# The first stage of a hybrid attention layer written as one fixed order, with value products of 512 columns and matmuls on a cleared tile at the start

## The chip, the cores and the metric

The kernel runs on one core of one Trainium2 chip. The metric is the device time of one execution in microseconds (us). TensorE (PE) does the matmuls and PEld loads their stationary operands; VectorE (DVE), ScalarE (ACT) and GpSimd (POOL) work elementwise; every DMA in this kernel is issued from SyncE's queue (SP). Operands live in on-chip memory, and matmul results in eight banks of PSUM of 128 x 512 fp32 each.

## The reference

One layer of a bidirectional encoder on 1024 tokens of width 1024, fp32. A normalised input `h` is projected once into everything; two kinds of attention run on parts of the projection, and their gated outputs are merged.

```
h = rmsnorm(x, attn_norm_g)
proj = h @ w_in
(c_q, c_kv, k_rope, z_mla, q_dil, k_dil, v_dil, z_dil,
 g_mla, g_dil) = split(proj)              # 256, 128, 32, 512, 3 x 1536, 512, 2 x 1024 columns
a_out = mla_attention(c_q, c_kv, k_rope, positions, ..., w_uq, w_ukv)   # 8 heads, low-rank q and kv
y_mla = (a_out * silu(z_mla)) @ w_o_mla
d_out = dilated_mixture(q_dil, k_dil, v_dil, positions)    # 3 groups of 8 heads, dilations 1, 4, 16
y_dil = (d_out * silu(z_dil)) @ w_o_dil
merged = sigmoid(g_mla + b[:1024]) * y_mla + sigmoid(g_dil + b[1024:]) * y_dil
out = rmsnorm(x + merged @ w_out, final_norm_g)
```

## The kernel before

Every fp32 operand is kept as two parts, a high one rounded to the matmul's format and a low one with the rest (`split`: a cast on ACT for the high part, a subtraction on DVE or POOL for the low one). A product of two such operands is three matmuls, high by high, high by low, low by high (`mm3`, lines 145 to 147).

The run has these stages. (1) *First products* (`latent_proj`): the 416 columns of `w_in` for the latents `c_q`, `c_kv` and `k_rope`, from the transposed input `hTh`/`hTl` (in the profile `at_r`) and the weights `wl_h`/`wl_l`, 8 pieces of 128 tokens, each over 8 pieces of the depth (`kc`): 192 matmuls. The first 512 tokens go depth by depth, as x and weights arrive, the second 512 token piece by token piece. `token_factors` takes the squares of the rows of x (line 276) and the reciprocal norm, as a column (`rcol`) and, by a transpose (line 280) and a trip through DRAM (`s_rs`), as a row `R`; `tables` makes the rotary tables. (2) *Latents* (`latents`): for each half of the tokens the latents are scaled on DVE (line 358), transposed on PE against an identity in `consts` (line 365), split (lines 368, 369), multiplied by the up-projections `uq`, `ukv`, and every result is put into a staging tile `mla_st` of 512 KB and stored to DRAM (`s_qn`, `s_qr`, `s_kn`, `s_kp`, `s_mv`). (3) *Values* (`dil_v`): for each of 3 groups and each of 2 quads of heads, 8 token pieces of 8 x 3 matmuls with 256 columns of value weights (`w_h`, `w_l`), scaled by `rcol` and stored from `dv_st` or `dv_s2`. (4) `block_sums` prepares sums and differences of the input, and `blocks` makes the other projections in 16 items of 7 products ("places") of 12 matmuls of 512 columns, in banks `st_a` to `st_d`; the weights of a place are prepared `LEAD` = 5 places ahead by `block_operand`. (5) Attention and output.

What sets the order: up to `blocks` the Tile framework's scheduler orders the instructions of each engine by a simulated timeline, so latents and value products are mixed as it sees fit; `blocks` and attention stand in a `manual_schedule`, in which each engine follows the order of the code. A tile pool with `bufs=n` gives a name n buffers in turn; the (n+1)th use waits until the first is free. The latents have 2 PSUM banks and 2 staging tiles, the value and first products 6 banks. Weight loads, loads of x, and all stores go through SP's one queue in that order.

```
    def run(self):
                ...
                with tc.tile_pool(name="pj_a", reuse_waits="tile", bufs=NB_A, space=PSUM) as pj, ...
                            self.latent_proj(lp, wl, xp, pj)
                            self.tables(xp)
                            self.token_factors(xp, pl)
                            ...
                                self.latents(up, lp, tp, pl)
                            self.dil_v(0, 0, vp, pj)
                            self.dil_v(0, 1, vp, pj)
```

Of the kernel before, what the change touches and what calls it, by code (L numbers as in the profile page):

```python
# [10 lines left out]
F32 = mybir.dt.float32  # L11
# [28 lines left out]
NB_A = 6  # L40
# [21 lines left out]
class Net:  # L62
# [127 lines left out]
    def constants(self, cp):  # L190
        nc, a = self.nc, self.a
        t = cp.tile([128, 1], F32, name="warm")
        nc.vector.memset(t, 0.0)
        nc.scalar.activation(out=t, in_=t, func=AF.Square)
        c = cp.tile([128, 156], F32, name="consts")
        self.dma(c, a["consts"])
        self.ident, self.ga, self.gq, self.hb, self.iv = c[:, 0:128], c[:, 128:136], c[:, 136:139], c[:, 139:155], c[:64, 155:156]
# [35 lines left out]
    def latent_proj(self, lp, wl, xp, pj):  # L233
# [9 lines left out]
        for half in range(2):  # L243
            ps = [pj.tile([128, 512], F32, name="pj") for _ in range(4)]
            todo = []
            for kc in range(8):
                self.load_x(half, kc, xp)
                if half == 0:
                    raw = wl.tile([128, 416], F32, name="wl_raw", bufs=3)
                    self.dma(raw, a["wl"][kc])  # L250
                    self.split(raw, h[:, kc], l[:, kc], nc.gpsimd if kc % 2 else v)
                for t in range(4):
                    todo.append((kc, t))
            if half:
                todo.sort(key=lambda x: x[1])
            for kc, t in todo:
                ts = slice(512 * half + 128 * t, 512 * half + 128 * t + 128)
                self.mm3(ps[t][:, :416], self.hTh[:, kc, ts], self.hTl[:, kc, ts], h[:, kc], l[:, kc], kc == 0, kc == 7)
            for t in range(4):
                i = 4 * half + t  # L260
                junk = xp.tile([128, 256], F32, name="x_junk", bufs=2)
                nc.scalar.activation(out=junk, in_=ps[t][:, 0:256], func=AF.Square, accum_out=self.lss[:, 0, i:i + 1])
                nc.scalar.activation(out=junk[:, 0:128], in_=ps[t][:, 256:384], func=AF.Square, accum_out=self.lss[:, 1, i:i + 1])
                v.tensor_copy(self.lat[:, i, 0:400], ps[t][:, 0:400])
                v.tensor_copy(self.lat[:, i, 416:432], ps[t][:, 400:416])
            if half == 0:
                v.tensor_scalar(out=self.hb, in0=self.hb, scalar1=0.5, scalar2=None, op0=ALU.mult)

    def token_factors(self, xp, pp):

        nc, a = self.nc, self.a
        ss = xp.tile([128, 8], F32, name="x_ss", bufs=1)
        for t in range(8):
            x = xp.tile([128, D], F32, name="x_in")
            self.dma(x, a["x"][128 * t:128 * t + 128, :])
            nc.scalar.activation(out=x, in_=x, func=AF.Square, accum_out=ss[:, t:t + 1])
        y = self.rsqrt(ss, 1.0 / D, xp, 8)
        nc.vector.tensor_copy(self.rcol, y)
        pt = pp.tile([128, 512], F32, name="pj")
        nc.tensor.transpose(pt[:8, :128], y, self.ident)  # L280
        row = xp.tile([8, 128], F32, name="x_row", bufs=1)
# [5 lines left out]
    def tables(self, tp):  # L287
# [4 lines left out]
        self.dma(pi, a["positions"].partition_broadcast(64))  # L292
        ang = tp.tile([64, S], F32, name="ang", bufs=1)
# [7 lines left out]
        v.tensor_scalar(out=ang, in0=ang, scalar1=PI_LO, scalar2=-PI_LO, op0=ALU.min, op1=ALU.max)  # L301
        cs = tp.tile([64, 2, S], F32, name="cs", bufs=1)
        nc.scalar.activation(out=cs[:, 1], in_=ang, func=AF.Sin)
        v.scalar_tensor_tensor(out=ang, in0=ang, scalar=-1.0, in1=ang, op0=ALU.mult, op1=ALU.max)
        v.tensor_scalar(out=ang, in0=ang, scalar1=-1.0, scalar2=float(np.float32(np.pi / 2)), op0=ALU.mult, op1=ALU.add)
        nc.scalar.activation(out=cs[:, 0], in_=ang, func=AF.Sin)
        self.dma(self.cst, cs)
# [7 lines left out]
    def rope(self, pa, pb, cos, sin, tp):  # L315
# [3 lines left out]
        m = [tp.tile([128, 512], F32, name=f"rope_m{i}") for i in range(4)]  # L319
# [6 lines left out]
    def up_weights(self, lp):  # L326
# [5 lines left out]
        for i in range(3):  # L332
            raw = lp.tile([128, 1024], F32, name="u_raw")
            n = 768 if i < 2 else 1024
            self.dma(raw[:, :n], a["wuq"][:, 768 * i:768 * i + 768] if i < 2 else a["wukv"])
            self.split(raw[:, :n], uh[:, i] if i < 2 else kh, ul[:, i] if i < 2 else kl, nc.gpsimd)
        return uh, ul, kh, kl

    def latents(self, up, lp, tp, pj):

        nc, a = self.nc, self.a
        v = nc.vector
        uh, ul, kh, kl = up
        for half in range(2):
            c512 = slice(half * 512, half * 512 + 512)

            r = self.rcol[:, 4 * half:4 * half + 4]
            sc = tp.tile([128, 2, 4], F32, name="lat_sc")
            for i in range(2):
                v.scalar_tensor_tensor(out=sc[:, i], in0=self.lss[:, i, 4 * half:4 * half + 4], scalar=(0.5, 1.0)[i], in1=r, op0=ALU.mult, op1=ALU.mult)  # L350
                v.tensor_tensor(out=sc[:, i], in0=sc[:, i], in1=r, op=ALU.mult)
            y = self.rsqrt(sc.rearrange("p a b -> p (a b)"), 1.0 / 128, tp, 8)
            for i in range(2):
                v.tensor_tensor(out=y[:, 4 * i:4 * i + 4], in0=y[:, 4 * i:4 * i + 4], in1=r, op=ALU.mult)
# [1386 lines left out]
```

## Time and profile before

| | |
|---|---|
| median of 3 runs | 1227.03 us (1226.45 to 1229.11) |
| the profiled execution | 1229.1 us, its span 1227.1 |
| PE busy in the span | 1204.8 us (98%), 6909 matmuls recorded |
| DVE, ACT, POOL busy | 729.4, 611.9, 579.1 us |
| first matmul | 5.76 us |
| first block product | 224.80 us |

Times in the profile are counted from the start of its span. A row of the waits names the engine and its instruction, what ended its idle time, and then the total, the number and the longest. A row of the timeline has the start, the duration (from issue to the modelled end, so matmuls in a row overlap; what one costs is the distance from its start to the next start), the engine, the line of the kernel, and output <- inputs; in square brackets stands the idle time before it. `at_r` is the transposed input, `pj` a bank of the first stage, `w_h` and `w_l` the weight parts.

### The profile page before, as it was taken

The page shows a single profiled execution, that of the slowest core. Times are in us where ns is not written, and L with a number is a line of the kernel's source. Part 1 is how long each engine was busy: PE and PEld are TensorE (multiplying, and loading weights), DVE is VectorE, ACT ScalarE, POOL GpSimd, SP SyncE. Part 2 cuts the span into 40 slices and gives each one's busy share as a digit, 9 for nine tenths or more (in the row PEclk, how much of TensorE's full clock was granted, in tenths as well). Part 3 has the DMA queues.
Part 4 walks back from the last instruction along what each step waited for, and adds up shares of the span by engine and source line. Part 5 has one row for each costly group of instructions (what it writes and reads, how often), then busy time and mean ns, then how long its engine had stood idle before and what let it go on. Part 6 is the DMA issues. An engine that isn't in the chain of part 4 may idle for free.

```text
span 1227.1 us, 19477 instructions
## 1 busy us (share of the span) xinstructions
PE 1204.8 (98%) x6909; PEld 1061.2 (86%) x6909; DVE 729.4 (59%) x1304; ACT 611.9 (50%) x1284; POOL 579.1 (47%) x490
## 2 busy tenths in 40 slices
PE   8989999999999999999999999999999999999997
PEld 7989999888888888888989898888888888888886
DVE  7483534376566753346666666647667767769442
ACT  6533335443434434446564756546556555654222
POOL 1361218777777777643365633416730101158322
PEclk9989999999999999999999999999999999999999
DMA  9858579356536544286889897965473445235241
GB/s 336 233 160 306 192 288 335 104 146 165 158 106 182 152 132 129 103 239 216 242 231 285 222 296 214 277 181 124 155 194 95 119 104 140 78 112 177 81 154 52
DMA packets 126416, 221.37 MB, mean 180 GB/s; under 512 B 28072, under 2 KB 60400, under 8 KB 121392
## 3 DMA queue, kind: packets, MB, share of 16 engines
q1 hardware_dynamic: 126320, 220.14, 60.4%
q8 instruction: 54, 0.88, 0.3%
q14 instruction: 42, 0.34, 0.1%
HBM read 149.24 MB, written 70.85 MB: 179 GB/s over the span
## 4 chain that ended last, share of the span: by engine, by line
PE 78%; DMA 9%; DVE 3%; ACT 3%; POOL 3%; issue 2%; SPq 1%; ACTq 0%; POOLq 0%; DVEq 0%
PE bank L145 6%; PE bank L147 6%; PE bank L146 6%; PE bank L871 4%; PE st_a L145 2%; PE st_a L147 2%; PE st_a L146 2%; PE st_c L146 2%; PE st_d L146 2%; PE st_d L145 2%; PE st_c L145 2%; PE st_d L147 2%; PE st_c L147 2%; PE bank L896 2%; PE bank L895 2%
## 5 line engine op out<-in xcount | busy, mean ns | idle before, releaser
L152 POOL TENSOR_TENSOR w_l<-w_raw,w_h 128x512 fp32r<-128x512 f32 x188 | 245.8, 1321 | 234.6 <-ACT w_h L151 183.2
L151 ACT CAST w_h<-w_raw 128x512 fp32r<-128x512 f32 x188 | 112.2, 620 | 106.3 <-POOL w_raw L496 90.6
L145 PE MATMUL bank<-at_r,w_h 128*128 128x512 f32 x344 | 141.3, 411 | 0.0
L146 PE MATMUL bank<-at_r,w_h 128*128 128x512 f32 x344 | 134.8, 392 | 0.6 <-POOL at_r L152 0.6
L147 PE MATMUL bank<-at_r,w_l 128*128 128x512 f32 x344 | 135.0, 392 | 0.0
L879 DVE TENSOR_TENSOR at_r<-bank,at_r 128x512 fp32r<-128x512 f32 x128 | 87.8, 687 | 68.0 <-ACT at_r L873 67.5
L873 ACT CAST at_r<-bank 128x512 fp32r<-128x512 f32 x128 | 74.9, 585 | 82.0 <-PE bank L871 81.2
L147 PE MATMUL pj<-w_h,at_r 128*128 128x256 f32 x384 | 109.7, 286 | 0.0
L146 PE MATMUL pj<-w_l,at_r 128*128 128x256 f32 x384 | 109.6, 286 | 0.0
L145 PE MATMUL pj<-w_h,at_r 128*128 128x256 f32 x384 | 109.6, 285 | 0.0
L496 POOL TENSOR_TENSOR w_raw<-w_raw 128x512 f32<-128x512 f32 x64 | 82.9, 1295 | 0.1
L871 PE MATMUL bank<-consts,at_f 128*128 128x128 f32 x512 | 76.8, 272 | 0.5 <-DVE at_r L879 0.5
L147 PEld LDWEIGHTS bank<-at_r,w_l 128*128 128x128 f32 x344 | 64.5, 188 | 14.5
L147 PEld LDWEIGHTS pj<-w_h,at_r 128*128 128x128 f32 x384 | 74.3, 194 | 1.0
L146 PEld LDWEIGHTS pj<-w_l,at_r 128*128 128x128 f32 x384 | 74.3, 193 | 0.8
L145 PEld LDWEIGHTS pj<-w_h,at_r 128*128 128x128 f32 x384 | 74.3, 193 | 0.7
L1144 DVE TENSOR_TENSOR at_r<-bank,at_r 128x512 fp32r<-128x512 f32 x64 | 43.9, 685 | 51.5 <-ACT at_r L1140 51.2
L146 PEld LDWEIGHTS bank<-at_r,w_h 128*128 128x128 f32 x344 | 65.0, 189 | 9.7 <-POOL at_r L152 1.0
L145 PEld LDWEIGHTS bank<-at_r,w_h 128*128 128x128 f32 x344 | 64.9, 189 | 8.8
L896 PE MATMUL bank<-at_r,at_r 128*128 128x256 f32 x256 | 66.9, 283 | 1.4 <-DVE at_r L879 1.4
L895 PE MATMUL bank<-at_r,at_r 128*128 128x256 f32 x256 | 66.9, 282 | 0.0
L1125 ACT ACTIVATE at_f<-at_f,at_f 128x256 f32<-128x256 f32 x128 | 64.1, 504 | 3.8 <-DVE at_f L1118 3.7
(325 smaller groups left out, 3328.2 us busy)
## 6 DMA issues: line engine op xcount, KB each, us to landing
w_raw<-wt SPq DMA_DIRECT2D x48, 512.0 KB, 3.7
at_r<-s_dq SPq DMA_DIRECT2D x32, 512.0 KB, 8.1
s_dk<-dq_st SPq DMA_DIRECT2D x80, 128.0 KB, 2.3
s_dv<-dv_st SPq DMA_DIRECT2D x32, 256.0 KB, 3.4
s_dq<-dq_st SPq DMA_DIRECT2D x64, 128.0 KB, 2.4
zt<-s_gt SPq DMA_DIRECT2D x32, 256.0 KB, 3.5
w_raw<-wv SPq DMA_DIRECT2D x12, 512.0 KB, 5.7
at_r<-s_dk SPq DMA_DIRECT2D x8, 576.0 KB, 10.3
```

Of the source, the lines that this page charges most:

```text
L145: mm(out, lh, rh, start=start, stop=False, skip_group_check=skip)
L146: mm(out, lh, rl, start=False, stop=False, skip_group_check=skip)
L147: return mm(out, ll, rh, start=False, stop=stop, skip_group_check=skip)
L151: self.nc.scalar.copy(out=h, in_=raw)
L152: sub.tensor_tensor(out=l, in0=raw, in1=h.bitcast(F32), op=ALU.subtract)
L496: self.nc.gpsimd.tensor_tensor(out=b[out], in0=b[x], in1=b[y], op=ALU.subtract)
L871: self.nc.tensor.transpose(pt[:, o:o + 128], self.P[k, b][:, 128 * kc:128 * kc + 128], self.ident)
L873: self.nc.scalar.copy(out=h, in_=pt)
L879: self.nc.vector.tensor_tensor(out=l, in0=pt, in1=h.bitcast(F32), op=ALU.subtract)
L895: mm(out, vv[:, kc], ph[:, x], start=kc == 0, stop=False)
L896: mm(out, vv[:, kc], pl[:, x], start=False, stop=kc == 7)
L1125: nc.scalar.activation(out=p, in_=p, func=AF.Exp, scale=-1.0, bias=nm, accum_out=den)
```

## The change

The whole run stands in a `manual_schedule`. `first_products` and `first_stage` replace `latent_proj`, `token_factors`, `dil_v` and the scheduler's mixing.

- The value products have 512 columns: both quads of a group together. `v_part` is half the depth of one token piece, 12 matmuls; 48 parts (`c` = 0 to 47) make the stage. A piece of 512 columns has two parts, which lie some parts apart.
- `latents` becomes a generator of 36 steps. From part 6 on, 1.75 steps are taken behind each part (`LATENTS_BEGIN`, `LATENTS_PACE`). The staging tile has 5 buffers. The scaling of the latents goes to parts 2 to 9, the copy of `R` to part 20 (`token_row`), `block_sums` to part 30 and on, the first five block operands to parts 44 to 47, on DVE.
- PSUM has two pools of 4 banks. The first products use both, then the values one and the latents the other.
- At the beginning PE does ten matmuls of 416 columns on a piece of `wl_h` that DVE clears (`idle`), into a bank that is overwritten later. The first depth piece has its twelve products ordered by operand: 4 high by high, 4 with the low weights, 4 with the low input. The weights' load stands ahead of x's; the cast of this first piece is on DVE. `consts` comes in two parts.
- Value weights are loaded in pieces of 256 KB. The rotary tables' four multiplies by `R` (line 1632), the stores of zeros and the masks' load move into `blocks`. The operands of the block products alternate between two pools by fours instead of by ones.

```
-        for half in range(2):
-            ps = [pj.tile([128, 512], F32, name="pj") for _ in range(4)]
...
+        idle = h[:, 7]
+        v.memset(idle.bitcast(F32), 0.0)
+        for _ in range(10):
+            nc.tensor.matmul(ps[7][:, :416], lhsT=idle[:, 0:128], rhs=idle, start=True, stop=True)
+        for kc in range(8):
+            raw = wl.tile([128, 416], F32, name="wl_raw", bufs=4)
+            if kc == 0:
+                x, c = xp.tile([128, 512], F32, name="x_t", bufs=6), slice(0, 512)
+                self.dma(raw, a["wl"][0])
+                self.dma(x, a["xt"][0, :, 0])
+                v.tensor_copy(h[:, 0], raw)
+                nc.scalar.mul(self.hTh[:, 0, c], x, self.ga[:, 0:1])
...
+                for i, (p, q) in enumerate(((self.hTh, h), (self.hTh, l), (self.hTl, h))):
+                    for t in range(4):
+                        nc.tensor.matmul(ps[t][:, :416], lhsT=p[:, 0, 128 * t:128 * t + 128], rhs=q[:, 0], start=i == 0, stop=False)
+                continue
...
+    def v_part(self, c, pool, tp):
+
+        g, r = divmod(c, 16)
+        part, t = divmod(r, 4)
+        t += 4 * (part // 2)
+        s = (0, 1, 1, 0)[part] ^ (g & 1)
+        begin = part % 2 == 0
+        if begin:
+            self.v_ps[t] = pool.tile([128, 512], F32, name="pj")
+        ps = self.v_ps[t]
+        sl = slice(128 * t, 128 * t + 128)
+        for i in range(4):
+            kc = 4 * s + i
+            self.mm3(ps, self.hTh[:, kc, sl], self.hTl[:, kc, sl], *self.v_w[s, i], begin and i == 0, not begin and i == 3)
...
+            pl = pool(ctx, "pj_l", 4, space=PSUM)
+            pj = pool(ctx, "pj_a", 4, space=PSUM)
...
+            latents = self.latents(next(weights), up, tp, pl)
...
+            for c in range(48):
+                self.v_part(c, pj, vp)
+                g, r = divmod(c, 16)
+                if 2 <= c < 10:
+                    self.latent_scaled(c - 2)
...
+                if c == 20:
+                    self.token_row(tp, pl)
...
+                if c >= LATENTS_BEGIN and latents:
+                    steps += LATENTS_PACE
+                    while steps >= 1 and latents:
+                        steps -= 1
...
+                            next(latents)
...
+                elif later and c >= 30:
+                    next(later, None)
...
+            if x in (2, 3, 4, 5):
+                y, c = (self.cos_d, self.sin_d)[x // 2 - 1], slice(512 * (x % 2), 512 * (x % 2) + 512)
+                self.nc.gpsimd.tensor_tensor(out=y[:, c], in0=y[:, c], in1=self.R[:, c], op=ALU.mult)
```

PE at the very beginning, before: three rows of the start and how they go on (line 145 is high by high, 146 the low weights, 147 the low input).

```order
L145 MATMUL pj<-wl_h,at_8192_r 128x416 x4
L146 MATMUL pj<-wl_l,at_8192_r 128x416
L147 MATMUL pj<-wl_h,at_8192_r 128x416
L146 MATMUL pj<-wl_l,at_8192_r 128x416
L147 MATMUL pj<-wl_h,at_8192_r 128x416
```

And in the changed kernel (lines 265 and 278 are its `first_products`):

```order
L265 MATMUL pj<-wl_h 128x416 x10
L278 MATMUL pj<-wl_h,at_8192_r 128x416 x4
L278 MATMUL pj<-wl_l,at_8192_r 128x416 x4
L278 MATMUL pj<-wl_h,at_8192_r 128x416 x4
L145 MATMUL pj<-wl_h,at_8192_r 128x416
L146 MATMUL pj<-wl_l,at_8192_r 128x416
```

Ten matmuls of the cleared tile now stand ahead, and the low products of the first depth piece are grouped by operand instead of alternating.

PE where the latents' transposes begin, before: `lat` is the scaled latents, `consts` the identity, and the products around it are values of 256 columns.

```order
L145 MATMUL pj<-w_h,at_8192_r 128x256
L146 MATMUL pj<-w_l,at_8192_r 128x256
L365 MATMUL pj<-consts,lat 128x128 x4
L147 MATMUL pj<-w_h,at_8192_r 128x256
L145 MATMUL pj<-w_h,at_8192_r 128x256
L365 MATMUL pj<-consts,lat 64x128 x4
L146 MATMUL pj<-w_l,at_8192_r 128x256
```

In the changed kernel, at the last transposes of the first half and the first up-projections behind them:

```order
L146 MATMUL pj<-w_l,at_8192_r 128x512
L147 MATMUL pj<-w_h,at_8192_r 128x512
L440 MATMUL pj<-consts,lat 64x128 x4
L145 MATMUL pj<-lat_h,uq_h 128x512
L146 MATMUL pj<-lat_l,uq_h 128x512
L147 MATMUL pj<-lat_h,uq_l 128x512
L145 MATMUL pj<-lat_h,uq_h 128x512
L146 MATMUL pj<-lat_l,uq_h 128x512
L147 MATMUL pj<-lat_h,uq_l 128x512
L145 MATMUL pj<-w_h,at_8192_r 128x512
```

The transposes and the up-projections now stand between whole parts of twelve value matmuls of 512 columns, no longer between single matmuls of 256. From the first block product on, PE's order is the same in both kernels.

SP in the first half of the latents, in the changed kernel: stores of the latents (`mla_st`), of the values (`dv_st`) and loads of value weights (`wv`).

```order
L141 DMA s_qn<-mla_st 256x1x512
L141 DMA s_qr<-mla_st 256x1x512
L141 DMA s_dv_68<-dv_st 128x1024
L141 DMA s_kn<-mla_st 256x1x512 x2
L141 DMA s_dv_68<-dv_st 128x1024
L141 DMA s_kn<-mla_st 256x1x512 x2
L141 DMA s_dv_68<-dv_st 128x1024
L141 DMA w_raw<-wv 128x2x256 x4
L141 DMA s_mv<-mla_st 128x1024
```

Before, a value store there was 128x512 (256 KB), twice as many of them, and a load of value weights was 128x1024.

More of the change, by code (lines that the diff above doesn't have):

```diff
@@ L38 @@
 GATES_END = PROJ_BEGIN = 33
-NB_A = 6
+LATENTS_BEGIN, LATENTS_PACE = 6, 1.75
 DIL = (1, 4, 16)
@@ L269, in token_factors, with product @@
-    def token_factors(self, xp, pp):
-        nc, a = self.nc, self.a
-        ss = xp.tile([128, 8], F32, name="x_ss", bufs=1)
[L273 to L276, printed above, removed]
+        ps = {}
+        def product(t, kc):
+            ts = slice(128 * t, 128 * t + 128)
+            self.mm3(ps[t][:, :416], self.hTh[:, kc, ts], self.hTl[:, kc, ts], h[:, kc], l[:, kc], kc == 0, kc == 7)
@@ new lines, in first_products, with load, squares @@
+        for kc in range(8):
+            self.load_x(1, kc, xp)
+        for t in range(4, 8):
+            for kc in range(8):
+                product(t, kc)
+        ss = xp.tile([128, 8], F32, name="x_ss", bufs=1)
+        xs = {}
+        def load(t):
+            xs[t] = xp.tile([128, D], F32, name="x_in")
+            self.dma(xs[t], a["x"][128 * t:128 * t + 128, :])
+        def squares(t):
+            nc.scalar.activation(out=xs[t], in_=xs[t], func=AF.Square, accum_out=ss[:, t:t + 1])
@@ new lines, in first_products @@
+        self.v_load(0, 0)
+        for t in range(3):
+            load(t)
+        next(tables)
+        for t in range(4):
+            squared(t)
+            taken(t)
+        for i in range(4):
+            self.v_split(0, i, nc.gpsimd)
+        for t in range(3):
+            squares(t)
+            if t < 2:
+                load(t + 3)
+        next(tables)
+        squared(4)
+        taken(4)
+        self.v_load(0, 1)
+        for t in range(5, 8):
+            squares(t - 2)
+            load(t)
+            if t == 5:
+                next(tables)
+            if t == 6:
+                for i in range(4):
+                    self.v_split(1, i, nc.gpsimd)
+            squared(t)
+            taken(t)
@@ L277, in token_factors, with token_row @@
+        for t in range(6, 8):
+            squares(t)
+        run_all(tables)
         y = self.rsqrt(ss, 1.0 / D, xp, 8)
-        nc.vector.tensor_copy(self.rcol, y)
+        v.tensor_copy(self.rcol, y)
+        v.tensor_scalar(out=self.hb, in0=self.hb, scalar1=0.5, scalar2=None, op0=ALU.mult)
+    def token_row(self, tp, pp):
+        nc = self.nc
         pt = pp.tile([128, 512], F32, name="pj")
-        nc.tensor.transpose(pt[:8, :128], y, self.ident)
-        row = xp.tile([8, 128], F32, name="x_row", bufs=1)
+        nc.tensor.transpose(pt[:8, :128], self.rcol, self.ident)
+        row = tp.tile([8, 128], F32, name="mla_st", bufs=5)
```

433 lines of the change are left out of this document (245 added, 188 removed).

## The prediction

> **What bounds the kernel now.** I began with the page's table of busy times, to see which engine is full, then cut the span into its stages, then asked what TensorE (PE) waited for in the stages that the change rewrites, and last read single matmuls in the timeline for their steps (start to next start).
>
> ```profile
> span 1227.1 us, 19477 instructions
> PE 1204.8 (98%) x6909; PEld 1061.2 (86%) x6909; DVE 729.4 (59%) x1304; ACT 611.9 (50%) x1284; POOL 579.1 (47%) x490
> ```
>
> PE is the bound of the whole run: 98% busy, 22 us idle. The rows below are the stages: start, first products, value products beginning, latents, the rest of the values, blocks, attention with output. Columns: stretch and its length, busy time and count on PE, PEld, DVE, ACT and POOL, granted clock, DMA share, GB/s.
>
> ```profile
> 0.00:5.76 5.76, 0.00 (x1) 0.00 (x1) 0.68 (x3) 2.66 (x5) 0.72 (x5) 1.00 0.61 191
> 5.76:44.80 39.04, 39.04 (x194) 38.41 (x195) 28.07 (x41) 30.86 (x68) 13.70 (x11) 1.00 0.90 319
> 44.80:82.00 37.20, 32.31 (x248) 31.57 (x247) 25.93 (x96) 13.25 (x33) 17.10 (x12) 0.91 0.71 192
> 82.00:180.00 98.00, 97.55 (x705) 92.17 (x704) 43.18 (x71) 37.36 (x70) 22.68 (x18) 1.00 0.68 251
> 180.00:224.80 44.80, 42.78 (x357) 42.58 (x356) 18.53 (x15) 27.22 (x52) 35.34 (x26) 1.00 0.82 275
> 224.80:531.00 306.20, 306.20 (x1344) 253.36 (x1345) 169.60 (x271) 126.89 (x240) 217.50 (x179) 0.99 0.50 139
> 531.00:1227.10 696.10, 686.91 (x4070) 603.14 (x4068) 443.39 (x810) 373.62 (x822) 272.01 (x243) 1.00 0.61 174
> ```
>
> The blocks (306 us) have no idle PE at all, and PE's order there and in attention stays as it is; only what lies ahead of 224.80 can move. There PE stands still 5.76 us at the start and a little more later. Its waits up to 240 us, in total, times and longest:
>
> ```profile
> PE pj L145 <- ACT wl_h L151: 5.8, 1, 5.8
> PE pj L365 <- DVE lat_l L369: 3.4, 1, 3.4
> PE st_a L145 <- ACT dv_s L457: 2.0, 1, 2.0
> PE pj L365 <- DVE lat L358: 1.2, 1, 1.2
> PE pj L145 <- DVE mla_st L152: 0.4, 1, 0.4
> PE pj L280 <- DVE rs_y L210: 0.3, 1, 0.3
> ```
>
> After the start that is 3.4+2.0+1.2+0.4+0.3 = 7.3 us: the latents' transposes waiting for the scaled latents, and the first block product waiting for a PSUM bank that the value products still hold. Two of these stalls are followed by a slower clock. The clock column of short stretches shows it (the first row's 1.00 can't be believed: the steps there are long, see below):
>
> ```profile
> 5.76:11.17 5.41, 5.41 (x16) 5.16 (x17) 4.00 (x7) 4.32 (x8) 1.21 (x1) 1.00 0.99 365
> 11.17:44.80 33.63, 33.63 (x180) 33.25 (x179) 24.07 (x35) 26.54 (x62) 12.49 (x10) 1.00 0.89 311
> 73.97:79.43 5.46, 5.46 (x26) 5.33 (x27) 3.25 (x6) 1.67 (x3) 4.64 (x5) 0.50 0.91 273
> 224.80:229.62 4.82, 4.82 (x14) 3.83 (x15) 0.69 (x1) 1.78 (x4) 3.10 (x3) 0.65 0.44 135
> 229.96:232.00 2.04, 2.04 (x10) 1.69 (x9) 0.00 (x0) 0.34 (x1) 1.29 (x1) 1.00 1.00 365
> ```
>
> **A, the value products at 512 columns.** 1152 matmuls of 256 columns become 576 of 512, the same products summed in the same way. A step of 256 columns: in the stretch 180.00:224.80 PE was busy 42.78 us with 357 of them, 0.1198 us each. A step of 512 where the weights also change at every matmul: the 9 whole steps of 229.96:232.00 take 2.04 us, 0.2267 each. So 1152 x 0.1198 = 138.0 becomes 576 x 0.2267 = 130.6: -7.4. The latents' matmuls of 512 are a second witness and step more slowly, 4 steps in 0.93 us, 0.2325 each:
>
> ```profile
> 82.14 0.40 PE L145 MATMUL pj<-lat_h,uq_h 128*128 128x512 f32 x1
> 83.07 0.39 PE L146 MATMUL pj<-lat_l,uq_h 128*128 128x512 f32 x1
> ```
>
> By that, 576 x 0.2325 = 133.9, a gain of only 4.1. I take the blocks' row, since their moving operand is also a split weight block that streams in while PE goes on; the ends are -7.4 and 0 (no gain at all, should the new operands add what the halved count saves). The Trainium skill's page "TensorE: Matmul & The Clock Gate" (part 1, "Wait — 56ns, not 53.3ns?") speaks against this term: a warm step is N/2.4 GHz plus some 2.5 ns, so by it 576 fewer matmuls give an estimated 1.4 us. The trace disagrees for these matmuls: 2 x 0.1198 - 0.2267 is 12.9 ns for each one dropped, five times that.
>
> **B, the stalls.** The change writes the order out: the latents' 36 steps begin behind the seventh value part and go in at 1.75 steps a part, so every transpose has value products ahead of it that need nothing from DVE; the last values use a bank ring of their own, so the first block product needs no bank of theirs. The 7.3 us go: -7.3. New waits are not in the trace of before. Their lower end is 0. Their upper end is a row-sum for the staging tile of the latents (idle time of engines before they could write it, by what ended it, us and times):
>
> ```profile
>   DMA s_qn<-mla_st: 9.5, 3
>   DMA s_kn<-mla_st: 9.1, 5
>   DMA s_qr<-mla_st: 4.9, 3
>   DMA s_mv<-mla_st: 3.1, 2
> ```
>
> That is 26.6 us in which ACT waited for a store to land, with two buffers. ACT was idle there anyway and PE did not feel it (97.55 of 98.00 us busy). Now there are five buffers, so a store may land three products later. I take +1.0, near the lower end, since PE's own idle in that stretch is 0.45 us even with two.
>
> What is late next: first the reciprocal norms at the beginning. Eight squares of x rows run on ACT behind the first products:
>
> ```profile
> L276 ACT ACTIVATE x_in<-x_in 128x1024 f32<-128x1024 f32 x8 | 8.5, 1063 | 2.9 <-DMA x_in<-x 2.9
> ```
>
> With PE at the sum below, first products end near 42.5 and the first transpose comes seven parts (7 x 12 x 0.2267 = 19.0 us) later, at 61.6; 8.5 us of squares, the norm and two scalings have to fit into that and do by a few us. Second, the transfers: each stored piece is 512 KB, 14 of them per half, with four value stores of 512 KB and 1 MB of value weights between: 10.5 MB in about 35 us (72 to 107), 300 GB/s. The trace's densest stretch (40 slices of 80 to 106 us) and one such store there:
>
> ```profile
> GB/s 25 50 353 139 359 321 101 170 343 353 337 107 6 148 262 0 0 0 35 416 391 407 410 340 25 6 0 378 410 403 410 413 397 19 403 388 6 25 186 406
> s_qn<-mla_st SPq DMA_DIRECT2D x4, 512.0 KB, 3.1
> ```
>
> Peaks are about 410 GB/s, so 300 fits, and a landing of 3.1 us is under the four products that a ring of five allows. On SP's queue all stores and weight loads stand in one line: a load of value weights that waits for POOL's split of the previous ones holds back the stores behind it, and the copy of the norm row after the twentieth part waits for its own store. That is where the +1.0 would come from, and more if it goes badly.
>
> **C, the half clock after the stalls.** 73.97:79.43 ran at 0.50, 5.46 x 0.50 = 2.7 lost; 224.80:229.62 at 0.65, 4.82 x 0.35 = 1.7 lost. Without the stalls both go: -4.4. It goes only if no new wait of about 2 us stands in their place: the second one followed an idle of 2.0 us. The Trainium skill's page "TensorE: Matmul & The Clock Gate" (part 1, "What's actually happening") has the clock fall after an idle window of about 3.4 us; here the trace disagrees, with 2.0 us being enough.
>
> **D, the beginning.** In 5.76:11.17 the 16 matmuls take 5.41 us, 0.338 each; in 11.17:44.80 the 180 take 33.63, 0.1868 each. The first sixteen should take 3.0, so 2.4 us are lost to the cold clock. Ten matmuls on a cleared tile can begin as soon as DVE has cleared it, and take ten cold steps, 3.4 us:
>
> ```profile
> 0.80 0.06 DVE L193 MEMSET warm<- 128x1 f32 x1 [0.80 <-PEq L1729]
> 1.17 0.42 SPq L141 DMA_DIRECT2D x_t<-xt  x1
> 1.63 0.43 SPq L141 DMA_DIRECT2D wl_raw<-wl  x1
> 4.56 0.72 ACT L230 ACTIVATE at_r<-x_t,consts 128x512 fp32r<-128x512 f32 x1 [2.34 <-DMA x_t<-xt]
> 5.18 0.52 ACT L151 CAST wl_h<-wl_raw 128x416 fp32r<-128x416 f32 x1
> ```
>
> So from about 1.2 to 4.7 PE is active. Before, the clock rose 5.4 us after the first matmul; now that is 6.6. First real product: x's load is now second in line, one issue (0.46 us) later, but the weights' cast is off ACT, 0.52 us: 5.76 stays. So 0.9 of the 5.4 us at half clock remain, 0.9/5.4 x 2.4 = 0.4 lost, if the idle of a microsecond between dummies and products doesn't matter; if it spoils a window, nothing is gained. The ends are -2.4 and 0; I take -1.5, past the middle. The operand order of the first twelve (four high by high, four with low weights, four with low x) lets PE start without the low parts, as it did before (the x4 group came first then, too): 0.
>
> **E, what moves elsewhere.** Into the blocks go four multiplies of the rotary tables on POOL, six stores of zeros and the masks.
>
> ```profile
> L1632 POOL TENSOR_TENSOR cs_d<-cs_d,at_f 128x512 f32<-128x512 f32 x4 | 6.2, 1569 | 19.3 <-DMA s_dv<-dv_st 19.3
> ```
>
> 6.2 us on a POOL that is busy 217.50 of 306.20 us, with block operands five places (5 x 12 x 0.2267 = 13.6 us) ahead of their product: hidden, 0; with that lead gone each would cost up to 1.6. DMA share there is 0.50, which covers the stores. The block operands made on DVE at the end of the values lie beside PE's work: DVE was busy 18.53 of 44.80 us there.
>
> **The sum.** -7.4 -7.3 +1.0 -4.4 -1.5 = -19.6. A count forward needs the transposes, whose number (32) stays:
>
> ```profile
> 131.75 0.60 PE L365 MATMUL pj<-consts,lat 128*64 128x128 f32 x4
> 132.10 0.36 PE L145 MATMUL pj<-w_h,at_r 128*128 128x256 f32 x1
> 132.31 0.28 PE L146 MATMUL pj<-w_l,at_r 128*128 128x256 f32 x1
> ```
>
> Four of them and one value matmul take 0.56 us, so four cost 0.44 and 32 cost 3.5. Counting forward instead: 5.8 + 0.4..0.9 cold + 192 x 0.1868 = 35.9 + 130.6 + 120 latents matmuls x 0.2325 = 27.9 + 3.5 + 1.0 of new waits gives a first block product at 205.1 to 205.6, against 224.8 before, 19.2 to 19.7, and the 1.7 of slow clock behind it: 20.9 to 21.4. I take -20.5 between the two. The profiled execution took 1229.1 (span 1227.1 and 2.0 around it), so 1208.6; it stands 2.1 above the median of the runs, 1227.03, against which the forecast is 1206.5.
>
> **The rivals.** (1) The values gain little from 512 columns. For: the latents' 0.2325. Against: the blocks' 1344 matmuls in 306.20 us. With 0.2325 the time is 1209.8; with no gain 1213.9. By the Trainium skill's rule ("TensorE: Matmul & The Clock Gate", as above) the estimated saving of 1.4 us would make it 1212.5, between these two. (2) Partial new waits, 5 to 12 us in place of 1.0, in the latents or behind SP's queue: 1210.5 to 1217.5. For: the order is fixed, so one late store holds everything behind it, and the scheduler's freedom to go around it is gone. Against: 300 of 410 GB/s. (3) The other side: the stores' landing comes onto PE. The latents need staging tile, bank and PE in a fixed order; if the ring's reuse stalls ACT, the bank isn't emptied, and PE's next value part stands behind the latents' product in line. If all 26.6 us that ACT waited come onto PE: 1206.5 + 25.6 = 1232.1, slower, and each wait of 2 us adds up to 1.7 of slow clock. It decides (over +0.2%, about what a measurement can tell from no change, 2.5 us) from 24 us of such waits. Against: five buffers for two. (4) The ten matmuls warm nothing: 1208.0, within the likeliest case.
>
> **How the numbers follow.** Likeliest case, stalls gone and at most 4 us new, 0.70, at 1202 to 1210; rival 1 0.08, rival 2 0.15, rival 3 0.07 of which 0.01 lands within 0.2%. Faster 0.70+0.08+0.15 = 0.93, same 0.01, slower 0.06. The low end is the forecast with no new wait (-1.0), the whole cold loss gone (-0.9) and the forward count's other 1 us, and a little for steps that are better than the row, 1202; the high end takes in rival 1 and most of rival 2, 1216.
>
> **What would show it.** A: value matmuls in steps of 0.227, not 0.2325. B: PE's waits between 44 and the first block product under 2 us in total, the first st_a matmul near 205. C: granted clock 1.00 throughout this stretch. D: steps of 0.19 from about 8 us on, not 11. E: no idle of PE in the blocks. Wrong it would be with PE waiting for mla_st or a DMA in the latents, a DMA share of 0.9 between 72 and 107, or a transpose that waits at 61.

## The result and the profile after

The changed kernel took 1215.87 us (median of 5 runs, 1214.05 to 1216.81) against 1228.64 of the kernel before in runs beside it: a ratio of 0.9894, with a 95% interval of 0.9879 to 0.991. On a second occasion it took 1215.31 against 1230.73, 0.9872 (0.9855 to 0.9889). It is faster by 1.1 to 1.3%, some 13 to 15 us; the forecast was 20.5 us less.

The page and the windows of the changed kernel, cut at the first real product, the first value product, the first block product and the first product of attention (columns as in the prediction):

```profile
span 1214.1 us, 18210 instructions
PE 1197.5 (99%) x6343; PEld 1030.1 (85%) x6343; DVE 739.8 (61%) x1289; ACT 606.1 (50%) x1259; POOL 557.5 (46%) x473
```

```profile
5.88:43.27 37.39, 36.87 (x192) 35.94 (x193) 30.86 (x41) 26.45 (x57) 12.56 (x7) 1.00 0.85 286
43.27:209.14 165.87, 163.91 (x730) 134.49 (x730) 93.00 (x164) 76.40 (x139) 48.82 (x35) 0.99 0.69 241
209.14:513.78 304.64, 304.64 (x1345) 252.26 (x1344) 171.74 (x273) 126.40 (x239) 222.97 (x183) 1.00 0.53 157
513.78:1214.08 700.30, 688.21 (x4069) 604.27 (x4067) 442.73 (x809) 374.62 (x824) 272.39 (x243) 1.00 0.61 174
```

The same cuts of before:

```profile
5.76:44.67 38.91, 38.91 (x192) 38.28 (x193) 28.07 (x41) 30.73 (x67) 13.57 (x11) 1.00 0.90 318
44.67:224.80 180.13, 172.77 (x1306) 166.44 (x1306) 87.64 (x181) 77.96 (x154) 75.25 (x54) 0.98 0.72 245
224.80:531.20 306.40, 306.40 (x1344) 253.53 (x1345) 169.78 (x271) 127.08 (x240) 217.50 (x179) 0.99 0.50 139
531.20:1227.13 695.93, 686.72 (x4069) 602.98 (x4067) 443.21 (x809) 373.42 (x822) 272.01 (x243) 1.00 0.61 174
```

Read as a ledger: the first value product comes 1.4 us earlier; values with latents take 14.3 less; the blocks 1.8 less, since the half clock at their start is gone; attention and output, where nothing was to move, 4.4 **more**. That is 13.1, and with 0.2 less around the span the two profiled executions differ by 1229.1 - 1215.87 = 13.2. Two places need an explanation. PE's waits in the whole first stage of the changed kernel:

```profile
PE pj L265 <- DVE wl_h L263: 1.4, 1, 1.4
PE pj L146 <- DVE w_l L152: 1.2, 2, 0.9
PE pj L145 <- ACT w_h L151: 0.7, 1, 0.7
PE pj L278 <- ACT at_r L273: 0.7, 1, 0.7
PE pj L146 <- DVE wl_l L152: 0.4, 1, 0.4
```

There is none in the latents; the 0.7 and 1.2 us for `w_h` and `w_l` are a new stall at 174 to 178 us. And in attention, where the largest group of waits grew, the changed kernel and before:

```profile
PE bank L1088 <- DVE at_r L1071: 4.2, 3, 2.1
```

```profile
PE bank L896 <- DVE at_r L879: 1.4, 2, 1.2
```

### The profile page after: what moved, and what is told of

Its sections match the earlier page's. It is cut to its first block, busy times and chain, and to the rows that moved or that the text cites. A ratio compares the mean times of both kernels' runs of the same rounds, so it can differ in the third digit from the quotient of the medians.

```text
span 1214.1 us, 18210 instructions
## 1 busy us (share of the span) xinstructions
PE 1197.5 (99%) x6343; PEld 1030.1 (85%) x6343; DVE 739.8 (61%) x1289; ACT 606.1 (50%) x1259; POOL 557.5 (46%) x473
## 4 chain that ended last, share of the span: by engine, by line
PE 89%; DMA 5%; POOL 2%; DVE 1%; ACT 1%; issue 1%; SPq 0%; POOLq 0%; ACTq 0%; DVEq 0%
PE bank L145 7%; PE bank L146 7%; PE bank L147 7%; PE pj L146 5%; PE pj L147 5%; PE pj L145 5%; PE bank L1063 4%; PE st_d L146 2%; PE st_a L146 2%; PE st_c L146 2%; PE st_c L147 2%; PE st_a L147 2%; PE st_d L147 2%; PE st_d L145 2%; PE st_a L145 2%; PE st_c L145 2%
## 5 line engine op out<-in xcount | busy, mean ns | idle before, releaser
L152 POOL TENSOR_TENSOR w_l<-w_raw,w_h 128x512 fp32r<-128x512 f32 x175 | 230.1, 1327 | 213.2 <-ACT w_h L151 164.5
L1065 ACT CAST at_r<-bank 128x512 fp32r<-128x512 f32 x128 | 74.9, 585 | 85.4 <-PE bank L1063 84.8
L146 PE MATMUL pj<-w_l,at_r 128*128 128x512 f32 x192 | 75.5, 393 | 1.2 <-DVE w_l L152 1.2
L145 PE MATMUL pj<-w_h,at_r 128*128 128x512 f32 x192 | 75.7, 394 | 0.7 <-ACT w_h L151 0.7
L147 PE MATMUL pj<-w_h,at_r 128*128 128x512 f32 x192 | 75.4, 392 | 0.0
L1332 ACT CAST at_r<-bank 128x512 fp32r<-128x512 f32 x64 | 37.5, 586 | 54.3 <-PE bank L1324 53.1
L1063 PEld LDWEIGHTS bank<-consts,at_f 128*128 128x128 f32 x512 | 59.3, 140 | 1.3 <-DVE at_r L1071 0.9
L1088 PEld LDWEIGHTS bank<-at_r,at_r 128*128 128x128 f32 x256 | 48.7, 190 | 10.2 <-DVE at_r L1071 5.1
```

The lines of the kernel that those rows point to most:

```text
L145: mm(out, lh, rh, start=start, stop=False, skip_group_check=skip)
L146: mm(out, lh, rl, start=False, stop=False, skip_group_check=skip)
L147: return mm(out, ll, rh, start=False, stop=stop, skip_group_check=skip)
L152: sub.tensor_tensor(out=l, in0=raw, in1=h.bitcast(F32), op=ALU.subtract)
L1063: self.nc.tensor.transpose(pt[:, o:o + 128], self.P[k, b][:, 128 * kc:128 * kc + 128], self.ident)
L1065: self.nc.scalar.copy(out=h, in_=pt)
```

## Experiments: the new stall in the value products

ACT's rows that lead to it, in the changed kernel. The first two casts of the last value weights wait 7.11 us for their transfer; the third and fourth stand behind four scalings for the block sums, which themselves wait 0.76 us for `y`:

```profile
169.46 1.14 ACT L151 CAST w_h<-w_raw 128x512 fp32r<-128x512 f32 x2 [7.11 <-DMA w_raw<-wv]
171.36 2.67 ACT L571 ACTIVATE y<-y,consts 128x512 f32<-128x512 f32 x4 [0.76 <-DMA y<-xt]
173.93 1.12 ACT L151 CAST w_h<-w_raw 128x512 fp32r<-128x512 f32 x2
```

PE reaches the third piece at 173.7 (one step behind the row's 173.48) and has to wait. The granted clock falls behind it; the windows are the 3.4 us with the stall, the 3.4 us after them, and a stretch in attention:

```profile
173.48 0.39 PE L147 MATMUL pj<-w_h,at_r 128*128 128x512 f32 x1
174.59 0.50 PE L145 MATMUL pj<-w_h,at_r 128*128 128x512 f32 x1 [0.72 <-ACT w_h L151]
175.98 0.50 PE L146 MATMUL pj<-w_l,at_r 128*128 128x512 f32 x1 [0.89 <-DVE w_l L152]
```

```profile
172.96:176.37 3.41, 1.79 (x7) 0.93 (x7) 1.80 (x2) 3.41 (x7) 2.18 (x2) 1.00 1.06 406
176.37:179.79 3.42, 3.07 (x8) 1.97 (x7) 2.85 (x3) 2.65 (x5) 3.26 (x3) 0.50 1.04 417
889.76:893.17 3.41, 3.41 (x12) 2.82 (x11) 2.50 (x4) 3.25 (x6) 0.00 (x0) 0.50 0.79 276
```

Half clock for 3.4 us, 1.7 lost, in the second and the third row (the third follows the second stall in attention). Two theories for the weights were tried, beside a repeat of the changed kernel (`again`, no edit).

> The load of the rotary table cs_d (1 MB in four transfers) is moved from value part 29 to part 41, behind the last value weights and the inputs of the block sums. Theory 1 (the weights of the last value parts land late because 1 MB stands ahead of them on the queue): they land about 2.5 us earlier, the casts of the third and fourth piece follow, the stall at 173 us and its 3.4 us of half clock go: first block product at 205.2 to 206 instead of 209.1, 3 to 4 us less time than the changed kernel. Theory 2 (the casts of the third and fourth piece are late because ACT stands behind the four scalings of the block sums' inputs): the stall stays within 1 us, unless those inputs land earlier too.

```
-                if c == 29:
+                if c == 41:
                     self.cos_d, self.sin_d = self.table(dpool, "cs_d", 0)
```

> The four scalings of the first block-sum inputs come two value parts later on ACT, behind the casts of the third and fourth piece of the last value weights; all transfers stay in their order. Theory 2 (ACT's order): the casts come at 170.6 and 171.2 us instead of 173.9 and 174.5, the stall goes or falls under 0.5 us, no half clock, first block product at 205.2 to 206, 3 to 4 us less time. Theory 1 (late landing): the casts of the first two pieces stay at 169.5 us and the stall stays at 1 us or more, since DVE's subtractions then follow each other too late.

```
         yield
         yield
+        yield
+        yield
         scaled(0)
```

ACT's rows of cs_late, then of cast_first:

```profile
166.29 1.14 ACT L151 CAST w_h<-w_raw 128x512 fp32r<-128x512 f32 x2 [3.43 <-DMA w_raw<-wv]
169.66 0.73 ACT L571 ACTIVATE y<-y,consts 128x512 f32<-128x512 f32 x1 [2.23 <-DMA y<-xt]
170.55 1.96 ACT L571 ACTIVATE y<-y,consts 128x512 f32<-128x512 f32 x3 [0.17 <-DMA y<-xt]
172.41 1.12 ACT L151 CAST w_h<-w_raw 128x512 fp32r<-128x512 f32 x2
```

```profile
168.38 1.14 ACT L151 CAST w_h<-w_raw 128x512 fp32r<-128x512 f32 x2 [6.78 <-DMA w_raw<-wv]
169.71 1.14 ACT L151 CAST w_h<-w_raw 128x512 fp32r<-128x512 f32 x2 [0.18 <-DMA w_raw<-wv]
170.75 2.56 ACT L571 ACTIVATE y<-y,consts 128x512 f32<-128x512 f32 x4
```

| | first value to first block product, us | PE's waits in it | time | ratio to before |
|---|---|---|---|---|
| changed kernel | 165.87 | 2.0 | 1215.87 | 0.9894 (0.9879 to 0.991) |
| again | 165.53 | 1.6 | 1215.31 | 0.9872 (0.9855 to 0.9889) |
| cs_late | 162.91 | 0.7 | 1212.97 | 0.9855 (0.9841 to 0.987) |
| cast_first | 161.71 | none | 1212.08 | 0.9845 (0.9828 to 0.9862) |
| both in one | 161.71 | none | 1210.70 | 0.9858 (0.983 to 0.9887) |

Theory 1 alone is not enough, though its edit takes 3.0 of the 4.2 us: with the load moved, the first weights land 3 us earlier and no half clock follows, but the third and fourth cast still stand behind the scalings (172.41) and 0.7 us of stall stays. Theory 2 held: the order on ACT alone takes the whole stall, 165.87 - 161.71 = 4.2 us with its half clock, and 3.2 us of time against `again` in the same session. (The load of the fourth group of inputs moves by two parts with that edit, too, but it is issued at 182 us, behind the stall.) Both together:

> cast_first and cs_late in one: theory, the stall of the last value weights is gone already by the casts, so nothing more than 0.5 us is won over cast_first.

Its stretch from the first value to the first block product is the same 161.71, so as expected the second edit adds nothing there. It, `cast_first`, `cs_late` and two kernels below are faster than both kernels of this case, at 1210.6 to 1213.0 us; they were measured on different occasions, so which of them is the fastest is not shown.

## Experiments: the staging ring, the value's width, the first microseconds

> The latents' staging tile has 3 buffers instead of 5. Theory (the latents' own four banks, and whole value parts between their products, keep PE apart from the stores): PE's waits in the latents stay under 1 us in total. Rival (the ring of five is what hides the 26 us in which ACT waited for stores before the change): 3 to 15 us of waits of PE, and that much more time.

```
-name="mla_st", bufs=5
+name="mla_st", bufs=3
```

PE's waits between the first value and the first block product were 1.6 us, all at the last value weights, as in the changed kernel, none in the latents; 1215.42 us, 0.9883 (0.9861 to 0.9904). The rival of the prediction in which stores' landing comes onto PE has nothing for it: ACT waited 19.3 us for stores here (10.4 s_kn, 6.7 s_qn, 1.3 s_qr, 0.9 s_mv), and PE felt none of it. With five buffers ACT waited 6.7.

> The changed kernel with its value products as pairs of 256 columns, in the same fixed order, otherwise the same. Theory: 0.1198 a step instead of 0.2267 for two, so the first stage is 7.4 us longer on PE, of which the stall at 173 us gives back about 3.5, since PE comes to it later: first block product 3.5 to 7.4 us later than in the changed kernel. By the Trainium skill's page on TensorE (2.5 ns a matmul, 576 more of them) it would be an estimated 1.4 us longer before the stall is counted. It also moves the loads of PE's code by half a piece: if their place makes the stalls of attention, attention is another than 700 to 702 us.

```
-            self.mm3(ps, self.hTh[:, kc, sl], self.hTl[:, kc, sl], *self.v_w[s, i], ...)
+            for q in (slice(0, 256), slice(256, 512)):
+                self.mm3(ps[:, q], ..., *(x[:, q] for x in self.v_w[s, i]), ...)
```

(Two accumulations share a bank here, with a start each, so the values are other numbers; what is issued and moved is what the edit says.) Its steps at the end of the value products:

```profile
204.81 0.28 PE L145 MATMUL pj<-w_h,at_r 128*128 128x256 f32 x1
206.50 0.28 PE L147 MATMUL pj<-w_h,at_r 128*128 128x256 f32 x1
```

These are the first and the last of fifteen in a row: 14 steps in 1.69 us, 0.1207; over each stretch of 20 us the median is 0.1200. From first value to first block product it took 170.97 us with 1.1 us of waits, 9.3 more than `cast_first`, which has no wait there, and 8.2 more with its own waits taken off. So the width is worth about the 7.4 us of the prediction or a little more (576 x (2 x 0.1200 - 0.2267) is 7.7), and not the estimated 1.4 us that the Trainium skill's page "TensorE: Matmul & The Clock Gate" (part 1, "Wait — 56ns, not 53.3ns?") would make it. The time is 1220.70 (0.9917, 0.9889 to 0.9946), 4.8 to 5.4 us over the changed kernel.

> The ten matmuls on the cleared tile are left out. Theory: the first products lose 2.4 us to the cold clock as before, but about 1.5 us of waits for x and weights, which the fast clock lays bare, are covered by it: the first value product comes 0.9 to 1.6 us later (44.2 to 44.9 instead of 43.3) and the time is that much longer. Rival (the ten matmuls are worth the whole of the cold loss): 2.4 us. Rival (nothing): 0.

```
-        for _ in range(10):
-            nc.tensor.matmul(ps[7][:, :416], lhsT=idle[:, 0:128], rhs=idle, start=True, stop=True)
```

The first value product came at 43.30 us, as in the changed kernel (43.27), not 0.9 to 1.6 us later. The time was 1216.22 against 1215.31 of `again`; that is 0.9 us, the lower end of what was expected, but the ranges overlap (1215.36 to 1217.67, 1214.67 to 1217.71), so no difference is shown. The timeline tells why the product came no later. In this execution the clock rose in the third group of products, 3 us after the first, where before it had taken 5.4:

```profile
5.48 1.75 PE L276 MATMUL pj<-wl_h,at_r 128*128 128x416 f32 x4 [5.48 <-ACT at_r L271]
7.03 1.59 PE L276 MATMUL pj<-wl_l,at_r 128*128 128x416 f32 x4
8.42 1.05 PE L276 MATMUL pj<-wl_h,at_r 128*128 128x416 f32 x4
9.31 0.35 PE L145 MATMUL pj<-wl_h,at_r 128*128 128x416 f32 x1
9.50 0.35 PE L146 MATMUL pj<-wl_l,at_r 128*128 128x416 f32 x1
9.69 0.35 PE L147 MATMUL pj<-wl_h,at_r 128*128 128x416 f32 x1
```

In the changed kernel it was high before the first product, but PE then waited for weights:

```profile
7.50 0.91 PE L278 MATMUL pj<-wl_h,at_r 128*128 128x416 f32 x4
8.53 0.46 PE L145 MATMUL pj<-wl_h,at_r 128*128 128x416 f32 x1
9.39 0.46 PE L146 MATMUL pj<-wl_l,at_r 128*128 128x416 f32 x1 [0.40 <-DVE wl_l L152]
9.68 0.35 PE L147 MATMUL pj<-wl_h,at_r 128*128 128x416 f32 x1
```

The fifteenth product, the last row of each, begins at 9.7 us in both. Over the profiles the first value product comes at 42.5 to 43.6 where the full clock begins at 8.8 us or earlier (eight of them, with and without the ten matmuls, a second one of before among them), at 43.8 with 9.45 (`cs_late`, which has the ten matmuls and half a microsecond of idle PE behind them), at 44.2 and 45.0 with 9.8 and 12.0 (`pad_pe` and `pad_all`, below), at 44.7 and 45.4 with 11.2 (before and `before_shift`). The changed kernel's 43.27 is 1.4 and 0.3 us earlier than the two profiles of before (44.67 and 43.58) and no earlier than `no_warm`. So the place where the clock rises decides, and the last section shows what that place goes with; a gain in time from the ten matmuls is not shown.

## Experiments: attention, where nothing was moved

> The changed kernel once more. In its first profile the attention and output (first product in a bank to the end of the span) took 700.3 us, 4.5 us more than the 695.9 of before with the same order of PE: two stalls of 1.9 and 2.1 us where DVE waits for the reciprocal row's transfer (s_rr), and a half-clock stretch of 3.4 us behind the second. Theory (a landing that varies from one execution to the next): another value than 700.3, between 695.9 and 700.3, the stalls smaller or at other places. Rival (the changed first stage causes it): 700 again, with both stalls at the same places. The stall of 3 us in the value products at 173 to 177 us must be there again in both.

The repeat had 702.3 us, outside what the theory allowed, with the two stalls at nearly the same places (1.47 us at 334.6, 2.65 at 377.0). The second profile of before had 696.7:

> The kernel before once more, for a second profile of its attention and output. If the 4 to 6 us by which every profile of the changed kernel and its variants has a longer attention (699.9 to 702.4 us from the first product in a bank to the end) are chance, this one lies near 700 too; if they belong to the change, it is 695 to 697 again, with stalls of 1.2 us or less.

It is hardly chance, then, though before has only two profiles: every profile of a kernel with the changed first stage has 698.4 to 704.1, the two of before have 695.9 and 696.7. Common to most of the long ones is a stall 332 to 335 us into attention. In the changed kernel it is this (the first row is DVE's wait for the reciprocal row's transfer, the second PE's wait for what DVE does next):

```profile
845.57 0.69 DVE L1636 TENSOR_TENSOR at_f<-at_f,at_f 128x512 f32<-128x512 f32 x1 [5.07 <-DMA at_f<-s_rr]
846.92 0.39 PE L1088 MATMUL bank<-at_r,at_r 128*128 128x256 f32 x1 [1.88 <-DVE at_r L1071]
```

The last two transfers of such rows before it are issued at the same place, 323 us into attention, in both kernels. The DMA view of the 3.5 us from 323.7 us on (queue and kind: packets, MB, share; then issues with the time to landing), the changed kernel and before:

```profile
q1 hardware_dynamic: 547, 0.79, 95.7%
q8 instruction: 1, 0.02, 2.4%
at_f<-s_rr SPq DMA_DIRECT2D x1, 128.0 KB, 8.2
```

```profile
q1 hardware_dynamic: 533, 0.81, 95.4%
at_f<-s_rr SPq DMA_DIRECT2D x1, 128.0 KB, 6.3
```

What stands out is one packet of 16 KB on the queue q8. That queue has 54 such packets in before, where the trace has 6909 matmuls (with a weight load each, 256 instructions a packet), and 50 after, with 6343 (254 a packet): so it was read as the load of PE's program. 566 matmuls less shift where in attention these loads fall. The theory was tested by moving them, with matmuls too small to matter.

> As cast_first, but instead of ten matmuls of 416 columns on the cleared tile there are 64 of 64 columns: about the same time, 54 matmuls and 54 weight loads more. PE's program is loaded by transfers of 16 KB on a queue of their own, 54 before and 50 after the change, about one every 128 matmuls. In the changed kernel and its variants one of them runs 324 to 327 us into the attention, on the transfers that the stall at 333 us waits for, and one at 370, ahead of the stall at 375; before, they ran at 310, 334 and 352. With 54 matmuls more they fall where they fell before. Theory (the code transfers' place): the stall at 333 us goes, attention and output 696 to 697.5 us instead of 700 to 702.4, and about 4 us less time than cast_first. Rival (chance, or something else of the first stage): 700 to 702, both stalls stay.

```
-        for _ in range(10):
-            nc.tensor.matmul(ps[7][:, :416], lhsT=idle[:, 0:128], rhs=idle, ...)
+        for _ in range(64):
+            nc.tensor.matmul(ps[7][:, :64], lhsT=idle[:, 0:128], rhs=idle[:, :64], ...)
```

A miss as a kernel: 64 small matmuls took 13.7 us and the first product came at 15.05; 1222.11 us (0.9941, 0.9921 to 0.996). The loads fell at 317 and 342, the stall at 333 went (0.35 us, at 339), and others grew, 1.8 at 17 and 1.5 at 108 us; attention took 704.1, with two stretches of half clock, where 696 to 697.5 was expected. So the next ones used 8 columns of moving data and 8 of weights:

> As cast_first, with 68 matmuls of 8 columns on the cleared tile at the start instead of ten of 416: PE's program has 58 matmuls more, so that the transfers of its code fall where they fell before the change, at about 310 and 334 us of the attention instead of 325. Of all nine profiles so far a stall of over 1.3 us at 333 us stands in those six that have such a transfer at 324 to 327 us, and none over 0.5 us in the other three (before, before2, shift54; v256 has none either, with transfers at 312 and 336). Theory: no stall over 0.5 us at 333; the stalls at 17 and 105 us, which come with other transfers (8 KB, the code of the other engines, 90 to 94 us), stay. Attention and output 699.5 to 701.5 us instead of 702.4. Rival (chance): the stall at 333 is there. The first products start by 5.9 us in any case.

> As pad_pe, and ACT, DVE, POOL and SP also get instructions without work in value parts 12 to 34 (46 squares of one number and 46 drains, 19 and 21 clearings of one number), so that each engine's program is as long up to the attention as it was before the change, up to whole transfers of its code. Theory (where the code's transfers fall makes the 4 to 6 us of attention): attention and output 695.5 to 697.5 us, no stall over 0.5 us at 105 and 333, 5 us less time than cast_first at its 702.4. Rival (something else of the first stage, or chance): 699 to 703 as in the seven profiles of the changed first stage. The first stage loses at most 1 us by the added instructions.

The edit that both have:

```
+        for _ in range(68):
+            nc.tensor.matmul(ps[7][:8, :8], lhsT=idle[:, 0:8], rhs=idle[:, 0:8], start=True, stop=True)
```

And the other way round, the stall put into the kernel before:

> The kernel before with 70 matmuls of 8 columns on a cleared tile at its very start, where PE waits for the first data anyway: its program on PE is so much longer that the transfers of its code fall where they fall in the changed kernel, at 324 to 327 us of the attention instead of 310. Theory (the place of the code's transfer makes the stall): a stall of 1.2 to 2 us appears at 332 to 334 us of the attention, where the two profiles of before have none over 0.5; attention and output 697.5 to 699 us instead of 695.9 and 696.7, that is 1 to 2 us more time, unless the first stage, which the scheduler orders a little otherwise, takes that back. Rival (the changed first stage in another way): no stall over 0.5 us there.

```
+                v.memset(idle.bitcast(F32), 0.0)
+                for _ in range(70):
+                    nc.tensor.matmul(ps[3][:8, :8], lhsT=idle[:, 0:8], rhs=idle[:, 0:8], start=True, stop=True)
```

The same 3.5 us in before_shift, and PE's waits in its attention (the stall came, with 1.18 us at the low end of what was expected):

```profile
q1 hardware_dynamic: 1024, 0.89, 94.7%
q8 instruction: 1, 0.02, 2.3%
```

```profile
PE bank L901 <- DVE at_r L884: 4.0, 3, 2.6
```

| profile | q8 load near 325 us | stall at 332 to 335 | stall at 372 to 377 | attention and output, us |
|---|---|---|---|---|
| before | 310, 334 | none | 1.17 | 695.9 |
| before2 | 310, 336 | 0.41 | 1.39 | 696.7 |
| before_shift | **324** | 1.18 | 2.61 | 699.2 |
| changed kernel | **324** | 1.88 | 2.11 | 700.3 |
| again | **326** | 1.47 | 2.65 | 702.3 |
| cs_late | **325** | 1.59 | 1.16 | 699.9 |
| cast_first | **325** | 1.31 | 2.39 | 702.4 |
| both | **325** | 1.45 | 1.57 | 700.7 |
| no_warm | **327** | 1.35 | 2.02 | 701.2 |
| ring3 | **326** | 1.77 | 1.91 | 699.7 |
| v256 | 312, 336 | none | 1.39 | 701.2 |
| shift54 | 317, 342 | 0.35 (at 339) | 1.56 (at 380) | 704.1 |
| pad_pe | 313, 338 | none | 0.76 | 698.4 |
| pad_all | 312, 336 | none | 2.04 | 698.8 |

For the stall at 333 us this is shown both ways: it comes where a load of PE's code lies at 324 to 327 us, and goes where it lies elsewhere, in either first stage. The landing of the reciprocal row goes with it: 7.5 to 8.2 us in the eight profiles with such a load, 6.1 to 6.7 in the six without. An earlier such transfer, issued 176 to 184 us into attention, shows the same less cleanly: 7.4 to 9.0 us in the same eight, where a load falls inside it, 5.8 to 8.5 in the six. How one packet delays 128 KB by more than its own 1.3 to 1.4 us the trace does not tell. The stall at 374 us is 0.8 to 2.7 with no clean split.

That the place of the loads costs the whole 4.4 us is not shown. With every engine's program padded to before's length, attention took 698.8, not the 695.5 to 697.5 that theory gave; with PE's alone (`pad_pe`) it took 698.4, less than the 699.5 to 701.5 expected. The stall at 105 us (0.4 to 1.5 us in six of the profiles above), which was to stay in `pad_pe`, was gone in both, so the padding of the other engines is not shown to do anything. A stall of 1.2 to 1.4 us at 17 us stayed in both, in `pad_all` also one of 2.0 at 375. `v256` and `shift54` have no stall at 333 us either, and took 701.2 and 704.1, with 2.1 and 1.8 us at 17 us. Half clock makes part of the spread, too: two stretches of 3.4 us in `cast_first` and `shift54`, none in `pad_pe`, `pad_all`, `ring3` and `v256`. Of the 4.4 us by which the changed kernel's attention is longer, 2.5 are waits of PE (5.5 against 3.0 us, the stall at 333 us 1.9 of them) and 1.7 the stretch of half clock; why the other stalls differ stays open.

In time the padding shows little: pad_pe 1211.61 (0.9866, 0.9842 to 0.9891), pad_all 1210.55 (0.9857, 0.9832 to 0.9882), both 1210.70 beside them; their clock rose only at 9.8 and 12 us, which took back 0.9 to 1.7 us at the start. before_shift took 1230.97 against 1229.29, 1.0017 (1.0001 to 1.0033).

## Why the prediction came out as it did

The time lies inside the range, 0.1 us below its upper end, and 9.4 us above the forecast. The direction and the gains of A, B and C held, but that the time lies inside is in part luck: it is outside the likeliest case (1202 to 1210, given 0.70) and in the band of rival 2 (1210.5 to 1217.5), without that rival's waits in the latents. 7.3 us of the gain in the profiled executions (20.5 forecast, 13.2 measured) are missing, and the median of before lay 1.6 us higher when it was taken again.

- **A** (-7.4): right. Value steps are 0.2267 and the latents' too, instead of the 0.2325 I counted, 0.7 us more gain: in the changed kernel, twelve products of each take 2.72 us from first start to the next first start. The rival of a small gain, and the 1.4 us by the Trainium skill's rule, fell with v256.

```profile
73.76 0.39 PE L145 MATMUL pj<-lat_h,uq_h 128*128 128x512 f32 x1
76.48 0.39 PE L145 MATMUL pj<-w_h,at_r 128*128 128x512 f32 x1
79.20 0.39 PE L145 MATMUL pj<-lat_h,uq_h 128*128 128x512 f32 x1
```

- **B** (-7.3): right, none of the old stalls is left. **New waits** (+1.0): mis-sized, and in another place. I put the risk on the latents, where there is none, and on SP's queue; it came on ACT, whose casts of the last weights stand behind scalings that wait for a transfer; 1 MB ahead of those weights on SP's queue had its part (`cs_late` takes 3.0 us of it). It measured 4.2 us: 2.0 of named waits, 1.7 of half clock; the rest is by estimate the overlap with the next matmul that each of three waits loses (a matmul lasts 0.39 us, its step is 0.23). I had written that half clock returns with a stall of about 2 us; the sum did not carry it.
- **C** (-4.4): the two stretches went, 2.7 and 1.7; two new ones of 1.7 came, one with the new stall and one in attention.
- **D** (-1.5): 1.4 in the two profiles (44.67 to 43.27), close by luck: against the second profile of before it is 0.3, and `no_warm` came as early without the ten matmuls. The clock rose at 5.71 us instead of the forecast 6.6. The time of its rise decided, and waits for data stood in place of the cold steps.
- **E** (0): right in the blocks, 304.64 us against 306.40 less 1.7. Wrong behind them: "only what lies ahead of 224.80 can move" is the step that failed. Attention cost 4.4 us more with the same order on PE: 2.5 in waits, of which the stall at 333 us (1.9) goes with the place of the code's loads, and 1.7 in the half clock behind the second stall. Why the other stalls differ stays open.

## What to carry to other kernels

When an order is written out by hand, follow each engine's queue, not only PE's and the DMA queue: a cast that feeds PE next stands behind whatever was written ahead of it, and if that waits for a transfer, PE waits too. A changed number of instructions moves the loads of the program in everything that follows, so an unchanged stage with a tight transfer may gain or lose a microsecond or two; leave room for that in a forecast, and compare such stages over several profiles before explaining them. And a stall of a microsecond or two can cost as much again through the clock.

## What was not expected of the hardware

- A single 16 KB load of PE's code (1.3 to 1.4 us at that place) near a transfer on which PE depends went with a stall of 1.2 to 1.9 us where there was none over 0.4, and with a landing of 7.5 to 8.2 us instead of 6.1 to 6.7.
- The full clock began between 5.0 and 12.0 us in profiles of nearly the same start; ten matmuls ahead did not always bring it early (9.45 in `cs_late`), and a stall of 2.0 to 2.1 us was followed by half clock in the kernel before and the changed one, but not in `pad_all` (2.04) or `ring3` (1.77 and 1.91). The recorded changes of the clock show an order in this. Within each of the fourteen executions, as long as PE has work, they lie whole multiples of 3.413 us apart (in the changed kernel 5.71, 176.37, 179.79, 889.76 and 893.17 us: 50, 1, 208 and 1 of them), at another offset from the start each time. Cut into stretches of this length, the traces have the clock rise only behind stretches in which PE was busy 2.92 us or more, and fall only behind those with 1.84 us or less: behind 15 of the 17 such stretches (the other two are `ring3` with 1.74 and `v256` with 1.75). (Matmuls' ends are modelled, so these bounds are rough.) In `cs_late` the half microsecond of idle PE behind the ten matmuls leaves 2.89 us of one stretch, and the clock stayed low for one more. The 2.1 us stall of the changed kernel lies in one stretch and leaves PE 1.30 us; that of `pad_all` lies across two and leaves 1.94 and 2.85, at full clock:

```profile
882.39:885.80 3.41, 1.94 (x11) 1.39 (x9) 0.78 (x2) 0.59 (x1) 0.00 (x0) 1.00 0.65 228
885.80:889.21 3.41, 2.85 (x18) 2.58 (x19) 3.39 (x5) 1.69 (x4) 0.00 (x0) 1.00 0.80 276
```

- A matmul of 64 columns whose weights are loaded anew at the start took 0.21 us (13.7 us for 64), so many of them do not fit ahead of the first product; with 8 columns of weights and of data, 68 of them were done 2.8 us ahead of the first product at 6.1 us. The 64 did not raise the clock either: PE was busy with them through more than three of the stretches of 3.413 us, and the clock rose at 18.7 us, 3.6 us after the first real product.
